# First norm copied once out of PSUM by ACT and DVE in turn, other order of sums and weights, decays one activation at a time

## The chip, the core and the metric

The kernel runs on one core of a Trainium2 chip. Five engines work side by side, each through its own instructions in order: TensorE (PE) multiplies matrices, VectorE (DVE), ScalarE (ACT) and GpSimd (POOL) work on tiles of 128 partitions, and SyncE (SP) issues most of the DMA transfers. They wait for one another by semaphores. The metric is the device time of one execution in microseconds (us), the median of several.

## The reference

One block of a hybrid network on x of 1024 tokens by 1024 features, in fp32. The parts that matter here, cut:

```python
h = rmsnorm(x, norm_mix_pre)                      # x * rsqrt(mean(x*x) + eps) * w
proj = h @ w_in                                   # 1024 x D_IN
(rq, rk, rv, rg, gq, gk, gv, gg, ga, sq, sk, sv, gate_logits) = split(proj)
...                                               # retention of rq, rk, rv
z = ga @ gla_w_alpha2 + gla_b_alpha               # ga: 16 columns, z: 4 heads x 128
log_a = maximum(log_sigmoid(z) / 16, -1)
b = cumsum(log_a)                                 # in each chunk, along the tokens
q_dec, k_inv = q * exp(b), k * exp(-b)            # the decays of the GLA branch
...                                               # GLA, sliding-window attention (sq, sk, sv)
merged = sum(sigmoid(gate_logits) * (branches @ w_branch))
x = x + rmsnorm(merged @ w_out, norm_mix_post)
x = x + rmsnorm(feed_forward(rmsnorm(x, norm_ffn_pre)), norm_ffn_post)
```

## The kernel before

Every fp32 operand is split into two parts, hi (rounded by ACT's copy) and lo (the rest, a subtraction on DVE), and each product is three matmuls: hi hi, hi lo, lo hi. `split(hi, lo, src)` does this for one tile; its two lines are L127 and L128 in the trace.

**The first norm.** x is loaded as eight tiles of 128 tokens, four to a half. `first_norm` squares a tile with a sum (ms), `rstd_of` makes two small POOL instructions of it (add eps, power of -0.5), and DVE scales the tile (xn). TensorE transposes xn in pieces of 128 columns into banks of PSUM (xps), so that bank k holds 128 features of 512 tokens. `first_split` writes the split of such a bank times the norm's weight straight out of PSUM: hi by ACT, lo by DVE (both called hT). `first_whole` writes it once more, whole (hf), on ACT, for the sums of below.

**The products.** All of x's projections come from class `Pairs`, which makes two columns of 128 weights at a time (a key) by seven products instead of eight: p1 to p7, each of four tiles deep, so twelve matmuls of 512 columns. There are 29 keys: one for the keys of sliding-window attention, four for its queries, four for q and k of retention, twenty for gates. The products need sums of the weights (`sums`: s2, s3; DVE subtracts, then a split) and sums of the tiles hf (class `Sums`: t2, t1, t3; `make("t2")` runs them). x, y and z are the banks that products accumulate in. `snap` copies a bank to SBUF (sn) before a later product goes on in it. `out` hands a finished piece to `in_out`, which scales or activates it and stores it. `steps()` is a generator, one `yield` after each product, and the first two keys are taken together.

**The SWA values.** `swa_values(t0)` makes v of the sliding-window attention and ga for two blocks of tokens from the first norm and the weights wsv, which `split_sv` splits in three pieces, the lo part on POOL. `vhl` is the split of its result.

**The decays.** For each of four heads `gla_gate` makes z by one matmul for each half of the tokens (96 deep, the three parts of the split in one), then on ACT exp and ln, on DVE a clamp and a scan along the tokens (cent, with its middle in mid and its end in end), on ACT again exp of end, of mid, and of cent and -cent (ed), which go to DRAM by POOL's queue. exp and ln lie in different tables of ACT, with an ACT_TABLE_LOAD between.

**What sets the order.** Of the first part (from the first norm to `swa_values(6)`) the engines PE, DVE, ACT and POOL keep the order in which the code is written: class `Ordered` marks every instruction issued while `e.on` is true, and all of them have line L76 in the trace. After that, Tile's scheduler orders the instructions, within the waits. The decays are hung into the loop over `steps`: all of a head's work is issued between two products, at steps 10, 17, 24 and 31; `tc.issue_after` keeps the ln after both exp. Tiles named with dt_ come from a pool of 45 buffers of 128 x 1024 fp32, which the weights (raw, wh, wl), x and xn, the sums and the decays (e, cent) share; tiles named with bt come from another of 18 buffers of half that width.

Of the kernel before, what the change touches and what calls it, by code (L numbers as in the profile page):

```python
# [11 lines left out]
AF = mybir.ActivationFunctionType  # L12
ALU = mybir.AluOpType
# [5 lines left out]
D = 1024  # L19
NT = S // P  # L20
NK = D // P
H = 4
# [10 lines left out]
EPS = 1e-6  # L33
# [13 lines left out]
V_PRE, V_RW, V_RB, V_GW, V_FFN, V_BA, V_SNK, V_R, V_CAUSAL = 0, 8, 16, 24, 32, 40, 44, 60, 68  # L47
# [32 lines left out]
def block_kernel(ctx: ExitStack, tc: tile.TileContext, x, vecs, rows, alpha2, w_in, w_branch,  # L80
                 w_out, w_gate, w_up, w_down, cst_in, out):
    nc = tc.nc
    pe, ve, se, po = (Ordered(tc, e) for e in (nc.tensor, nc.vector, nc.scalar, nc.gpsimd))
# [15 lines left out]
    def bt(n, dt=F32):  # L99
        return bp.tile([P, TH], dt, name=f"{n}_{nid()}", tag="b")  # L100
# [7 lines left out]
    def bpair(n):  # L108
        t = dt_(n, F32R)
        return t[:, :TH], t[:, TH:]  # L110
# [21 lines left out]
    vec = const.tile([P, NVEC], F32, name="vec")  # L132
# [45 lines left out]
    def split_sv(raws):  # L178
        res = []
        for raw, kn in raws:  # L180
            wh, wl = wt_pair()
            split(wh[:, :kn * NSV], wl[:, :kn * NSV], raw[:, :kn * NSV], po)
            res += [(wh[:, k * NSV:(k + 1) * NSV], wl[:, k * NSV:(k + 1) * NSV]) for k in range(kn)]
        return res
# [111 lines left out]
            xs.append(xt)  # L296
        return xs

    def first_norm(xt, on_ve):
        xn = dt_("xn")  # L300
        ms = sm("ms", 1)
        if on_ve:
            ve.tensor_tensor_reduce(out=xn, in0=xt, in1=xt, scale=1.0 / D, scalar=0.0,
                                    op0=ALU.mult, op1=ALU.add, accum_out=ms)
        else:
            se.activation(out=xn, in_=xt, func=AF.Square, scale=1.0 / 32.0, accum_out=ms)
        r = rstd_of(ms, 1, EPS)
        ve.tensor_scalar(out=xn, in0=xt, scalar1=r, scalar2=None, op0=ALU.mult)
        return xn

    def first_whole(k, th, ps):
        hf[k][th] = bt("hf")
        se.activation(out=hf[k][th], in_=ps, func=AF.Copy, scale=vec[:, V_PRE + k:V_PRE + k + 1])

    def first_split(k, th, ps):
        xT[k][th] = bpair("hT")
        g = vec[:, V_PRE + k:V_PRE + k + 1]
        se.activation(out=xT[k][th][0], in_=ps, func=AF.Copy, scale=g)
        ve.scalar_tensor_tensor(out=xT[k][th][1], in0=ps, scalar=g, in1=xT[k][th][0],
                                op0=ALU.mult, op1=ALU.subtract)  # L320


    ga = const.tile([P, NT, RANK], F32, name="ga")
# [289 lines left out]
    def gla_gate(h):  # L613
        es, cents = halves(dt_("e")), halves(dt_("cent"))
        mid = const.tile([P, NT], F32, name=f"mid{h}")
        end = const.tile([P, NT], F32, name=f"end{h}")
        for th in range(2):
            ps = bank("z")
            pe.matmul(ps, lhsT=gate_in["a"][:96, h * DK:(h + 1) * DK], rhs=gate_in[th][:96, :],
                      start=True, stop=True)  # L620
            e = es[th]
            ve.tensor_scalar(out=e, in0=ps, scalar1=vec[:, V_BA + h:V_BA + h + 1], scalar2=-25.0,
                             op0=ALU.add, op1=ALU.max)
            last = se.activation(out=e, in_=e, func=AF.Exp, scale=-1.0)
        with tc.issue_after(last.ins):
            for e in es:
                se.activation(out=e, in_=e, func=AF.Ln, bias=1.0)
        for th in range(2):
            e = es[th]
            ve.tensor_scalar(out=e, in0=e, scalar1=-1.0 / 16.0, scalar2=-1.0, op0=ALU.mult, op1=ALU.max)  # L630
            b = cents[th]
            ve.tensor_tensor_scan(out=b, data0=gate_in["scan"], data1=e, initial=0.0, op0=ALU.mult, op1=ALU.add)
            b3 = b.rearrange("p (c t) -> p c t", c=4)
            m_ = mid[:, th * 4:(th + 1) * 4]
            ve.tensor_copy(out=m_, in_=b3[:, :, MID])
            ve.tensor_tensor(out=b3, in0=b3, in1=m_.unsqueeze(2).broadcast_to([P, 4, P]), op=ALU.subtract)
# [61 lines left out]
    xs = load_x(0)  # L698
# [5 lines left out]
    engines = (pe, ve, se, po)  # L704
    for e in engines:
        e.on = True
    xns = [first_norm(xt, False) for xt in xs]
    inp.blocks(ikeys[0])
    pss = [bank("xps") for _ in range(NK)]
    for j in range(4):  # L710
        for k in range(NK):
            pe.transpose(out=pss[k][:, j * P:(j + 1) * P], in_=xns[j][:, k * P:(k + 1) * P], identity=ident)
    for k in range(NK):
        first_split(k, 0, pss[k])
        if k < 2:
            first_whole(k, 0, pss[k])
    wsv = split_sv(wsv)
    next(steps)
    next(steps)
    xns = [first_norm(xt, j > 1) for j, xt in enumerate(xs2)]  # L720
    for k in range(2, NK):
        first_whole(k, 0, pss[k])
    swa_values(0)
    for k in range(NK):
        ps = bank("xps")
        for j in range(4):
            pe.transpose(out=ps[:, j * P:(j + 1) * P], in_=xns[j][:, k * P:(k + 1) * P], identity=ident)
        first_split(k, 1, ps)
        first_whole(k, 1, ps)
    inp.sums(ikeys[0])  # L730
    swa_values(2)
    inp.blocks(ikeys[1])
    next(steps)
    next(steps)
    swa_values(4)
    swa_values(6)
    for e in engines:
        e.on = False
    del xs, xs2, xns, pss
    wsv = None  # L740
    for k in range(KH):
        for z in range(2):
            po.dma_start(out=hTd[k][:, z * TH:(z + 1) * TH], in_=xT[k][1][z].bitcast(F32))
        xT[k][1] = None
    for i, _ in enumerate(steps):
# [18 lines left out]

    dist = bt("dist")[:, :2 * W]
    sp.dma_start(out=dist, in_=cst_in[:, C_DIST:C_DIST + 2 * W])
    po.tensor_scalar(out=nsnk, in0=snk, scalar1=-1.0, scalar2=None, op0=ALU.mult)


    keys, queries, biases = {}, {}, {}  # L770
# [620 lines left out]
```

## Time and profile before

| | |
|---|---|
| median of 3 runs | 2230.72 us (2230.05 to 2232.22) |
| the profiled execution | 2227.39 us, its span 2225.6 us |
| TensorE's granted clock, mean over the span | 0.98 |
| PE busy | 2118.2 us, 95% of the span, 10660 matmuls |
| DVE busy | 1202.5 us, 54% |
| ACT busy | 917.1 us, 41% |
| POOL busy | 241.0 us, 11% |
| DMA | 364.06 MB, mean 164 GB/s |

The profile is of one execution. Its own time stands beside the span since the time holds a little work around the span. Busy shares are averages over stages: in the first tenth of the span PE is busy for half to nine tenths of each slice, later for nearly all. Times within the trace count from the start of the span. "Idle before <- releaser" says how long the engine waited ahead of an instruction, and for whose instruction.

### The profile page before, as it was taken

The numbers are of one execution on the slowest core, as the hardware profiler recorded it, in microseconds if no ns is written. First come the engines' busy times: TensorE is split into PE (matmuls) and PEld (weight loads), VectorE is DVE, ScalarE is ACT, GpSimd is POOL, SyncE is SP. The second block draws the span as 40 slices with busy tenths as digits, with TensorE's granted clock in tenths as the row PEclk, the third lists the DMA queues.
The fourth block names the chain that finished last, engine by engine and source line by source line (L and its number), as shares of the span: only waits on it lengthen the run. The fifth ranks groups of instructions, "written<-read, shape, count | busy, mean of one in ns | idle before, by whom it ended". The sixth has DMA issues, their size and how long they took to land. (4 is left out here: it accounts for less than half of the span.)

```text
span 2225.6 us, 28749 instructions
## 1 busy us (share of the span) xinstructions
PE 2118.2 (95%) x10660; PEld 1792.9 (81%) x10660; DVE 1202.5 (54%) x2215; ACT 917.1 (41%) x1776; POOL 241.0 (11%) x413
## 2 busy tenths in 40 slices
PE   5688999999999999999989999998899999999998
PEld 5567788888889999999967888877688888878786
DVE  3666754444427986655554344426565555544351
ACT  5345444444437775444333212145433333333140
POOL 3011000000012222333321000031000000000000
PEclk9898999999999999999999999999999999999999
DMA  5277655555575446766564535332365555464451
GB/s 184 68 218 224 204 172 161 163 163 166 169 221 173 145 148 210 259 218 204 190 255 156 160 110 156 104 122 87 89 171 142 139 140 142 127 239 164 152 189 38
DMA packets 343277, 364.06 MB, mean 164 GB/s; under 512 B 16464, under 2 KB 267728, under 8 KB 343136
## 3 DMA queue, kind: packets, MB, share of 16 engines
q1 hardware_dynamic: 299776, 265.20, 39.6%
q10 hardware_dynamic: 30816, 54.02, 6.6%
q0 software_dynamic: 12544, 43.00, 5.0%
q8 instruction: 84, 1.38, 0.3%
q14 instruction: 57, 0.47, 0.1%
HBM read 264.64 MB, written 97.52 MB: 163 GB/s over the span
## 5 line engine op out<-in xcount | busy, mean ns | idle before, releaser
L128 DVE TENSOR_TENSOR wl<-raw,wh 128x1024 fp32r<-128x1024 f32 x131 | 160.1, 1223 | 158.2 <-ACT wh L127 80.8
L127 ACT CAST s<-raw 128x512 fp32r<-128x512 f32 x202 | 122.5, 620 | 243.1 <-DVE raw L384 79.8
L127 ACT CAST wh<-raw 128x1024 fp32r<-128x1024 f32 x141 | 147.3, 1047 | 155.0 <-DMA raw<-in_w_down 55.2
L409 PE MATMUL x<-t,s 128*128 128x512 f32 x408 | 161.7, 401 | 21.4 <-ACT sn L359 12.6
L410 PE MATMUL x<-t,s 128*128 128x512 f32 x408 | 163.1, 400 | 0.9 <-DVE t L128 0.7
L411 PE MATMUL x<-t,s 128*128 128x512 f32 x408 | 162.3, 398 | 0.0
L242 PE MATMUL pf<-o,wh 128*128 128x512 f32 x384 | 148.1, 393 | 8.4 <-ACT o L127 8.4
L243 PE MATMUL pf<-o,wh 128*128 128x512 f32 x384 | 149.7, 392 | 0.2 <-DVE o L128 0.2
L359 ACT COPY sn<-x 128x512 f32<-128x512 f32 x151 | 88.4, 586 | 144.5 <-PE x L411 134.9
L257 PE MATMUL v<-wh,hT 128*128 128x256 f32 x512 | 146.4, 286 | 0.0
L259 PE MATMUL v<-wh,hT 128*128 128x256 f32 x512 | 145.4, 284 | 0.0
L258 PE MATMUL v<-wl,hT 128*128 128x256 f32 x512 | 145.4, 284 | 0.0
L1322 PE MATMUL dn<-wh,f 128*128 128x512 f32 x352 | 137.0, 392 | 3.7 <-ACT f L127 3.7
L128 DVE TENSOR_TENSOR s<-raw,s 128x512 fp32r<-128x512 f32 x202 | 136.2, 688 | 2.1 <-ACT s L127 1.5
L1323 PE MATMUL dn<-wl,f 128*128 128x512 f32 x352 | 137.1, 391 | 0.0
L245 PE MATMUL pf<-o,wl 128*128 128x512 f32 x384 | 121.1, 390 | 0.0
L1191 POOL TENSOR_TENSOR rr<-rr,mhalf 128x1 f32<-128x1 f32 x16 | 8.7, 541 | 959.4 <-DVE rr L1190 959.4
L409 PEld LDWEIGHTS x<-t,s 128*128 128x128 f32 x408 | 78.7, 194 | 40.7 <-ACT sn L359 14.3
L1325 PE MATMUL dn<-wh,f 128*128 128x512 f32 x352 | 109.1, 390 | 0.0
L257 PEld LDWEIGHTS v<-wh,hT 128*128 128x128 f32 x512 | 98.7, 193 | 1.2
L258 PEld LDWEIGHTS v<-wl,hT 128*128 128x128 f32 x512 | 98.8, 193 | 1.1
L259 PEld LDWEIGHTS v<-wh,hT 128*128 128x128 f32 x512 | 98.7, 193 | 0.1
(303 smaller groups left out, 5365.8 us busy)
## 6 DMA issues: line engine op xcount, KB each, us to landing
raw<-in_w_in SPq DMA_DIRECT2D x138, 512.0 KB, 6.1
raw<-in_w_down SPq DMA_DIRECT2D x44, 512.0 KB, 6.8
raw<-in_w_gate SPq DMA_DIRECT2D x43, 512.0 KB, 4.8
raw<-in_w_up SPq DMA_DIRECT2D x43, 512.0 KB, 4.7
v<-v POOLq DMA_DIRECT2D x32, 512.0 KB, 4.0
v<-v SPq DMA_DIRECT2D x32, 512.0 KB, 6.5
gT<-go ACTq DMA_DIRECT2D x48, 256.0 KB, 3.9
raw<-in_w_branch SPq DMA_DIRECT2D x24, 512.0 KB, 6.0
```

The lines of the kernel that those rows point to most:

```text
L127: se.copy(out=hi, in_=src)
L128: return (eng or ve).tensor_tensor(out=lo, in0=src, in1=hi, op=ALU.subtract)
L242: pe.matmul(p_, lhsT=wh, rhs=hi, start=(k == 0), stop=False)
L243: pe.matmul(p_, lhsT=wh, rhs=lo, start=False, stop=False)
L257: pe.matmul(ps, lhsT=lh, rhs=rh, start=start, stop=False)
L258: pe.matmul(ps, lhsT=lh, rhs=rl, start=False, stop=False)
L259: pe.matmul(ps, lhsT=ll, rhs=rh, start=False, stop=stop)
L409: pe.matmul(ps, lhsT=h, rhs=hi, start=(start and k == 0), stop=False, skip_group_check=True)
L410: pe.matmul(ps, lhsT=h, rhs=lo, start=False, stop=False, skip_group_check=True)
L411: pe.matmul(ps, lhsT=l, rhs=hi, start=False, stop=(k == KH - 1), skip_group_check=True)
L1322: pe.matmul(ps[ch], lhsT=fh[:, ts_], rhs=ws[ch][0], start=(first and i == 0), stop=False)
L1323: pe.matmul(ps[ch], lhsT=fh[:, ts_], rhs=ws[ch][1], start=False, stop=False)
```

## The change

In the first norm:

- `first_norm` is taken apart into `first_square` and `first_scale`. All eight squares are on ACT now (before, two of them were on DVE), four of them between the tiles of the first half.
- `first_whole` is gone. `first_split` copies a bank out of PSUM once, whole, to hf: even k on ACT, odd k on DVE. The split is made from hf in SBUF, hi on ACT and lo on DVE.
- `split_sv` (the SWA weights) is written after the first two products instead of before them.
- `blocks` of the second key (the cast of its weights) is written between the tiles of the second half. The second key's sums and t2 are put in front of `swa_values(4)` and (6).
- nsnk, a small POOL instruction that needs vec and that only the attention reads later, is put at the end of the ordered part.

In the decays, `gla_gate` becomes a generator with a `yield` behind each activation or pair of them, and `all_decays` runs the four heads one behind the other. The loop over `steps` takes one piece after each product from step 9 on; `issue_after` chains each activation to the end of the one kept in `last`.

```diff
-    def first_norm(xt, on_ve):
+    def first_square(xt):
...
-        if on_ve:
-            ve.tensor_tensor_reduce(out=xn, in0=xt, in1=xt, scale=1.0 / D, scalar=0.0,
-                                    op0=ALU.mult, op1=ALU.add, accum_out=ms)
-        else:
-            se.activation(out=xn, in_=xt, func=AF.Square, scale=1.0 / 32.0, accum_out=ms)
-        r = rstd_of(ms, 1, EPS)
+        se.activation(out=xn, in_=xt, func=AF.Square, scale=1.0 / 32.0, accum_out=ms)
+        return xn, rstd_of(ms, 1, EPS)
+
+    def first_scale(xt, xn, r):
         ve.tensor_scalar(out=xn, in0=xt, scalar1=r, scalar2=None, op0=ALU.mult)
         return xn
...
     def first_split(k, th, ps):
+        h = hf[k][th] = bt("hf")
+        g = vec[:, V_PRE + k:V_PRE + k + 1]
+        if k % 2:
+            ve.tensor_scalar(out=h, in0=ps, scalar1=g, scalar2=None, op0=ALU.mult)
+        else:
+            se.activation(out=h, in_=ps, func=AF.Copy, scale=g)
         xT[k][th] = bpair("hT")
-        g = vec[:, V_PRE + k:V_PRE + k + 1]
-        se.activation(out=xT[k][th][0], in_=ps, func=AF.Copy, scale=g)
-        ve.scalar_tensor_tensor(out=xT[k][th][1], in0=ps, scalar=g, in1=xT[k][th][0],
-                                op0=ALU.mult, op1=ALU.subtract)
+        split(*xT[k][th], h)
...
             last = se.activation(out=e, in_=e, func=AF.Exp, scale=-1.0)
-        with tc.issue_after(last.ins):
-            for e in es:
-                se.activation(out=e, in_=e, func=AF.Ln, bias=1.0)
+            yield
+        for e in es:
+            with tc.issue_after(last.ins):
+                last = se.activation(out=e, in_=e, func=AF.Ln, bias=1.0)
+            yield
...
             ve.tensor_copy(out=end[:, th * 4:(th + 1) * 4], in_=b3[:, :, P - 1])
-        se.activation(out=end, in_=end, func=AF.Exp)
-        se.activation(out=mid, in_=mid, func=AF.Exp)
+            yield
+        with tc.issue_after(last.ins):
+            se.activation(out=end, in_=end, func=AF.Exp)
+            se.activation(out=mid, in_=mid, func=AF.Exp)
+        yield
...
-                se.activation(out=o, in_=cents[th], func=AF.Exp, scale=sgn)
+                with tc.issue_after(last.ins):
+                    se.activation(out=o, in_=cents[th], func=AF.Exp, scale=sgn)
                 po.dma_start(out=ed[h][z][:, th * TH:(th + 1) * TH], in_=o)
+                yield
...
     for k in range(NK):
         first_split(k, 0, pss[k])
-        if k < 2:
-            first_whole(k, 0, pss[k])
-    wsv = split_sv(wsv)
+        if k % 4 == 3:
+            sq += [first_square(xt) for xt in xs2[k // 2 - 1:k // 2 + 1]]
+    xns = [first_scale(xt, *q) for xt, q in zip(xs2, sq)]
     next(steps)
     next(steps)
-    xns = [first_norm(xt, j > 1) for j, xt in enumerate(xs2)]
-    for k in range(2, NK):
-        first_whole(k, 0, pss[k])
+    wsv = split_sv(wsv)
     swa_values(0)
...
         first_split(k, 1, ps)
-        first_whole(k, 1, ps)
+        if k == 3:
+            inp.blocks(ikeys[1])
     inp.sums(ikeys[0])
     swa_values(2)
-    inp.blocks(ikeys[1])
     next(steps)
     next(steps)
+    inp.sums(ikeys[1])
+    inp.make("t2")
     swa_values(4)
     swa_values(6)
+    po.tensor_scalar(out=nsnk, in0=snk, scalar1=-1.0, scalar2=None, op0=ALU.mult)
...
-        if i in (10, 17, 24, 31):
-            gla_gate(len(gates_gla))
+        if i > 8:
+            next(decays, None)
```

DVE, where key 1's sums and t2 stand against the SWA values of the last four blocks. raw_215 and raw_216 are key 1's weights, s its sums, t those of the tiles hf; vhl_687 and vhl_745 (before) are the last two results of `swa_values`, vhl_601 (after) is that of `swa_values(2)`. Before:

```order
L76 TENSOR_TENSOR wl_606<-raw_215,wh_605 128x1024
L384 TENSOR_TENSOR raw_215<-raw_215,raw_216 128x512
L388 TENSOR_TENSOR raw_216<-raw_216 128x512
L76 TENSOR_TENSOR vhl_687<-sv_637,vhl_687 128x4x64
L76 COPY ga<-sv_637 128x16
L76 TENSOR_TENSOR vhl_687<-sv_638,vhl_687 128x4x64
L76 COPY ga<-sv_638 128x16
L76 TENSOR_TENSOR vhl_745<-sv_695,vhl_745 128x4x64
L76 COPY ga<-sv_695 128x16
L128 TENSOR_TENSOR s_118_762<-raw_215,s_118_762 128x512
L76 TENSOR_TENSOR vhl_745<-sv_696,vhl_745 128x4x64
L76 COPY ga<-sv_696 128x16
```

After:

```order
L76 TENSOR_TENSOR vhl_601<-sv_551,vhl_601 128x4x64
L76 COPY ga<-sv_551 128x16
L76 TENSOR_TENSOR vhl_601<-sv_552,vhl_601 128x4x64
L76 COPY ga<-sv_552 128x16
L76 TENSOR_TENSOR raw_215<-raw_215,raw_216 128x512
L76 TENSOR_TENSOR s_112_638<-raw_215,s_112_638 128x512
L76 TENSOR_TENSOR raw_215<-raw_216,raw_215 128x512
L76 TENSOR_TENSOR s_113_642<-raw_215,s_113_642 128x512
L76 TENSOR_TENSOR raw_216<-raw_216 128x512
L76 TENSOR_TENSOR raw_215<-raw_215 128x512
L76 TENSOR_TENSOR t_114_647<-hf_506,hf_462 128x512
L76 TENSOR_TENSOR t_114_647<-t_114_647,hf_291 128x512
```

The sums of key 1 and the first of t2 have moved in front of the last two SWA results, and the key's wl has moved up among the tiles, out of these rows.

ACT, at the end of the first head's decays: sn_1346 (before) and sn_1328 (after) are the same copy of bank x after p6 of the fourth key, wh_1348 and wh_1335 the next key's weights, ed the decays. Before:

```order
L643 ACT_TABLE_LOAD
L643 ACTIVATE ed_1250<-cent_1225 128x512
L675 ACTIVATE qs_1315<-sn_1125 128x512
L127 CAST s_217_1320<-raw_1022 128x512
L679 DMA sq_151<-qs_1315 128x512
L639 ACTIVATE mid_1226<-mid_1226 128x8
L638 ACTIVATE end_1227<-end_1227 128x8
L643 ACTIVATE ed_1253<-cent_1225 128x512
L643 ACTIVATE ed_1256<-cent_1225 128x512
L643 ACTIVATE ed_1259<-cent_1225 128x512
L127 CAST a22h_1298<-raw_1023 128x512
L359 COPY sn_1346<-x_1206 128x512
```

After:

```order
L127 CAST s_213_1297<-raw_1023 128x512
L683 DMA sq_151<-qs_1292 128x512
L356 COPY sn_1328<-x_1215 128x512
L640 ACT_TABLE_LOAD
L640 ACTIVATE mid_1209<-mid_1209 128x8
L639 ACTIVATE end_1210<-end_1210 128x8
L127 CAST wh_1335<-raw_1110 128x1024
L356 COPY sn_1376<-x_1215 128x512
L646 ACTIVATE ed_1384<-cent_1208 128x512
L127 CAST s_223_1355<-raw_1110 128x512
L356 COPY sn_1400<-x_1387 128x512
L646 ACTIVATE ed_1405<-cent_1208 128x512
```

The copy sn has moved in front of the table load and of all ed, and the four ed lie apart, with casts and copies between them.

PE, at the first gate product: z<-g,a is the first half of the first head; x_967 (before) and x_968 (after) are the bank of the third key in its product p4 with a22, and x_1215 is the next key's bank, whose product stands in front of p4 before. Before:

```order
L411 MATMUL x_967<-b_930,a22l_1095 128x512
L409 MATMUL x_967<-b_933,a22h_1094 128x512
L410 MATMUL x_967<-b_933,a22h_1094 128x512
L411 MATMUL x_967<-b_933,a22l_1095 128x512
L619 MATMUL z_1228<-g_192_1158,a_190_1148 128x512
L409 MATMUL x_967<-b_936,a22h_1094 128x512
L410 MATMUL x_967<-b_936,a22h_1094 128x512
```

After:

```order
L408 MATMUL x_968<-b_931,a22l_1096 128x512
L406 MATMUL x_968<-b_934,a22h_1095 128x512
L616 MATMUL z_1211<-g_192_1159,a_190_1149 128x512
L406 MATMUL x_1215<-hT_293,wh_1128 128x512
L407 MATMUL x_1215<-hT_293,wh_1128 128x512
L408 MATMUL x_1215<-hT_293,wl_1129 128x512
L406 MATMUL x_1215<-hT_298,wh_1128 128x512
```

Seven matmuls of the product with a22 now stand in front of the gate product, where nine of it and the next key's twelve stood.

## Rows read from the trace of the kernel before

**Rows 1.** Busy time of each engine by stretches, columns as in the first row

```profile
core 0: us, PE busy (x) PEld busy (x) DVE busy (x) ACT busy (x) POOL busy (x), PEclk, DMA share, GB/s
160.00:170.00 10.00, 3.21 (x9) 2.38 (x8) 7.42 (x14) 6.03 (x12) 3.78 (x7) 0.78 1.02 330
400.00:650.00 250.00, 250.00 (x1105) 207.01 (x1104) 112.67 (x161) 107.60 (x172) 4.78 (x2) 1.00 0.57 172
```

**Rows 2.** Waits of PE, first 110 us: line, releaser, us in total, times, longest

```profile
PE x L409 <- ACT t L127: 5.6, 1, 5.6
PE z L409 <- ACT s L127: 4.9, 1, 4.9
PE x L76 <- ACT wh L76: 4.5, 1, 4.5
...
PE x L76 <- DVE wl L76: 1.2, 1, 1.2
```

**Rows 3.** Timeline, 0 to 20 us: start, us, engine, line, operation, idle before

```profile
9.15 1.06 ACT L76 ACTIVATE xn<-x 128x1024 f32<-128x1024 f32 x1
9.53 0.29 POOL L767 TENSOR_SCALAR nsnk<-vec 128x16 f32<-128x16 f32 x1 [8.71 <-DMA vec<-in_vecs]
...
14.77 0.57 POOL L76 TENSOR_TENSOR rstd<-rstd,mhalf 128x1 f32<-128x1 f32 x1
...
16.55 0.69 ACT L76 ACTIVATE hT<-xps,vec 128x512 fp32r<-128x512 f32 x1 [4.22 <-PE xps L76]
```

**Rows 4.** Timeline of ACT and DVE, first tile of the second half

```profile
39.71 0.69 ACT L76 ACTIVATE hT<-xps,vec 128x512 fp32r<-128x512 f32 x1 [2.17 <-PE xps L76]
...
40.43 0.75 DVE L76 SCALAR_TENSOR_TENSOR hT<-xps,vec,hT 128x512 fp32r<-128x512 f32 x1 [0.31 <-ACT hT L76]
...
41.21 0.69 ACT L76 ACTIVATE hf<-xps,vec 128x512 f32<-128x512 f32 x1 [0.82 <-DVE hT L76]
41.80 0.68 ACT L76 ACTIVATE hT<-xps,vec 128x512 fp32r<-128x512 f32 x1
```

**Rows 5.** Timeline, 25 to 57 us: single instructions of POOL, DVE and ACT

```profile
25.14 5.10 POOL L76 TENSOR_TENSOR wl<-raw,wh 128x816 fp32r<-128x816 f32 x3 [9.80 <-ACT wh L76]
...
55.70 0.68 DVE L76 TENSOR_TENSOR raw<-raw,raw 128x512 f32<-128x512 f32 x1
...
56.42 0.62 ACT L76 CAST s<-raw 128x512 fp32r<-128x512 f32 x1
```

**Rows 6.** Timeline of PE, 102 to 217 us: where it waits

```profile
102.13 0.80 PE L409 MATMUL z<-t,s 128*128 128x512 f32 x1 [4.88 <-ACT s L127]
...
147.78 0.47 PE L619 MATMUL z<-g,a 96*128 96x512 f32 x1 [1.09 <-DVE g L606]
...
167.04 0.80 PE L409 MATMUL x<-t,s 128*128 128x512 f32 x1 [6.79 <-ACT sn L359]
...
168.06 0.63 PE L411 MATMUL x<-t,s 128*128 128x512 f32 x1
168.49 0.63 PE L409 MATMUL x<-t,s 128*128 128x512 f32 x1
...
192.48 0.50 PE L409 MATMUL x<-t,s 128*128 128x512 f32 x1 [3.12 <-ACT sn L359]
...
216.48 0.60 PE L409 MATMUL x<-t,s 128*128 128x512 f32 x1 [2.52 <-ACT sn L359]
```

**Rows 7.** Timeline of ACT, 155 to 167 us, in the first head's decays

```profile
155.34 1.28 ACT L627 ACT_TABLE_LOAD   x1
156.63 1.16 ACT L627 ACTIVATE e<-e 128x512 f32<-128x512 f32 x2
...
164.35 1.65 ACT L643 ACTIVATE ed<-cent 128x512 f32<-128x512 f32 x3
...
166.41 0.57 ACT L359 COPY sn<-x 128x512 f32<-128x512 f32 x1
```

**Rows 8.** DMA issues: line, queue, count, KB each, median us to landing

```profile
raw<-in_w_in SPq DMA_DIRECT2D x138, 512.0 KB, 6.1
```

More of the change, by code (lines that the diff above doesn't have):

```diff
@@ L297, in load_x @@
         return xs
-    def first_norm(xt, on_ve):
+    def first_square(xt):
         xn = dt_("xn")
         ms = sm("ms", 1)
-        if on_ve:
-            ve.tensor_tensor_reduce(out=xn, in0=xt, in1=xt, scale=1.0 / D, scalar=0.0,
-                                    op0=ALU.mult, op1=ALU.add, accum_out=ms)
-        else:
-            se.activation(out=xn, in_=xt, func=AF.Square, scale=1.0 / 32.0, accum_out=ms)
-        r = rstd_of(ms, 1, EPS)
+        se.activation(out=xn, in_=xt, func=AF.Square, scale=1.0 / 32.0, accum_out=ms)
+        return xn, rstd_of(ms, 1, EPS)
+    def first_scale(xt, xn, r):
         ve.tensor_scalar(out=xn, in0=xt, scalar1=r, scalar2=None, op0=ALU.mult)
         return xn
-    def first_whole(k, th, ps):
-        hf[k][th] = bt("hf")
-        se.activation(out=hf[k][th], in_=ps, func=AF.Copy, scale=vec[:, V_PRE + k:V_PRE + k + 1])
     def first_split(k, th, ps):
+        h = hf[k][th] = bt("hf")
[4 more added lines that the diff above has]
+            se.activation(out=h, in_=ps, func=AF.Copy, scale=g)
         xT[k][th] = bpair("hT")
-        g = vec[:, V_PRE + k:V_PRE + k + 1]
-        se.activation(out=xT[k][th][0], in_=ps, func=AF.Copy, scale=g)
-        ve.scalar_tensor_tensor(out=xT[k][th][1], in0=ps, scalar=g, in1=xT[k][th][0],
-                                op0=ALU.mult, op1=ALU.subtract)
+        split(*xT[k][th], h)
     ga = const.tile([P, NT, RANK], F32, name="ga")
@@ L706, in block_kernel @@
         e.on = True
-    xns = [first_norm(xt, False) for xt in xs]
+    xns = []
+    for xt in xs:
+        xns.append(first_scale(xt, *first_square(xt)))
     inp.blocks(ikeys[0])
@@ L712, in block_kernel @@
             pe.transpose(out=pss[k][:, j * P:(j + 1) * P], in_=xns[j][:, k * P:(k + 1) * P], identity=ident)
+    sq = []
     for k in range(NK):
         first_split(k, 0, pss[k])
-        if k < 2:
-            first_whole(k, 0, pss[k])
-    wsv = split_sv(wsv)
+        if k % 4 == 3:
+            sq += [first_square(xt) for xt in xs2[k // 2 - 1:k // 2 + 1]]
+    xns = [first_scale(xt, *q) for xt, q in zip(xs2, sq)]
     next(steps)
     next(steps)
-    xns = [first_norm(xt, j > 1) for j, xt in enumerate(xs2)]
-    for k in range(2, NK):
-        first_whole(k, 0, pss[k])
+    wsv = split_sv(wsv)
     swa_values(0)
@@ L728, in block_kernel @@
         first_split(k, 1, ps)
-        first_whole(k, 1, ps)
+        if k == 3:
+            inp.blocks(ikeys[1])
     inp.sums(ikeys[0])
     swa_values(2)
-    inp.blocks(ikeys[1])
     next(steps)
     next(steps)
+    inp.sums(ikeys[1])
+    inp.make("t2")
     swa_values(4)
     swa_values(6)
+    po.tensor_scalar(out=nsnk, in0=snk, scalar1=-1.0, scalar2=None, op0=ALU.mult)
     for e in engines:
         e.on = False
-    del xs, xs2, xns, pss
+    del xs, xs2, xns, pss, sq
     wsv = None
@@ L744, in block_kernel, with all_decays @@
         xT[k][1] = None
+    def all_decays():
+        for h in range(H):
+            yield from gla_gate(h)
+    decays = all_decays()
     for i, _ in enumerate(steps):
@@ L766, in block_kernel @@
     sp.dma_start(out=dist, in_=cst_in[:, C_DIST:C_DIST + 2 * W])
-    po.tensor_scalar(out=nsnk, in0=snk, scalar1=-1.0, scalar2=None, op0=ALU.mult)
     keys, queries, biases = {}, {}, {}
```

## The prediction

> **What bounds the kernel now.** I read the table by stretches first. Its column for PE says where the end of the run is decided: from 400 to 650 us, and at both sides of that stretch, TensorE is busy for all of the time, one matmul in 250/1105 = 0.226 us, while between 160 and 170 us it is busy for 3.21 us of 10, at 0.78 of its clock [rows 1]. The matmuls are the same in both programs, and from some 260 us on the two programs stand in the same order on every engine. So what TensorE idles less in the first 260 us, the whole run is shorter by, and the change can gain nothing anywhere else. Next the waits of TensorE in the first 110 us say which engine it idles for: the casts of ACT that end the chain of sums (t, s) and the weights of the second key (wh, wl) [rows 2]. Then I went through the timelines, engine by engine, for what stands ahead of these on ACT, DVE and POOL [rows 3 to 5], and for the stalls of TensorE from 100 to 220 us [rows 6] with the rows of ACT before them [rows 7]. Everything below is made against the profiled run, 2227.4 us; the median of the runs shown is 3.3 us above it, which I add at the end.
>
> **The start.** The last of the four sums of squares is there when ACT's square of 9.15 us has been read out, near 10.3 us, but POOL ends the last rstd at 14.77 + 0.57 = 15.3 us, because its first instruction, nsnk, waits 8.71 us for vec and all four rstd stand behind it [rows 3]. With nsnk at the end of the section POOL keeps pace with ACT, and the last rstd comes 1.4 us after the last sum, at 11.7 us: 3.6 us earlier. The row does not show what else POOL would do in these 8.71 us (in both programs one more instruction stands ahead of its first arithmetic, and the trace has no duration for it), so the other bound is a gain of nothing. I take 3.6, since ACT and PE show no other wait at that place. The first copy of a tile then starts at 16.55 - 3.6 = 12.9 us.
>
> **The tiles of the first norm.** Before, a tile of the second half takes 41.80 - 39.71 = 2.09 us: ACT writes hi out of PSUM, DVE the rest, and the whole copy on ACT waits 0.82 us for DVE [rows 4]. Eight tiles are 16.7 us, up to 56.4 us [rows 5]. After, a pair of tiles goes ACT copy 0.69, ACT cast 0.62 [rows 4, 5], DVE subtract 0.68 [rows 5], DVE copy of the odd tile (nearest row: its pass over PSUM, 0.75 [rows 4]), ACT cast 0.62, since DVE's copy of the odd tile stands behind its subtract for the even one. That is 3.36 us less the small overlaps at each start, about 3.3 us a pair instead of 4.2. In the first half two pairs, two squares on ACT and two pairs more end near 30 us, and the split of the SWA weights, which now stands behind the two products, lets POOL write the first wl (5.10 us for three [rows 5], 1.9 for the first) only by 34.5 us. The values of SWA are 48 matmuls of 272 columns, in proportion 0.12 us each and twice that after a stall, so some 8 us, and, with the transposes behind them, the first tile of the second half starts at 43.5 us instead of 39.71 [rows 4]: this part alone **loses 3.8 us**. The second half (13.2 us, and 0.95 us for the cast of key 1's weights in its middle) ends at 58 us.
>
> **Key 1, its sums and t2.** Before, x of key 1 waits 4.5 us for wh and 1.2 us for wl [rows 2]; after, both are done in the middle of the tiles. The products start as TensorE comes to them, about 57 us, last 24 x 0.226 = 5.4, and the last 96 matmuls of the SWA values (12.1 us) end at 75 us. Before, DVE then makes the rest of key 1's sums and t2, because they stand behind the SWA values; PE waits 5.6 us for t [rows 2]. After, DVE starts on them at 58: six sums of key 0 and six of key 1, each waiting twice for ACT's cast (5.3 us a key), 0.8 us of SWA values between, and t2 with its share of t1, twenty instructions of 0.6 us (0.68 less the overlap [rows 5]): 12.1 us and 1.2 at its start. 58.3 + 5.3 + 0.8 + 5.3 + 13.3 = 83 us, and t2's product ends at 84.5 us. The next product, z, started at 102.13 us after 4.88 us of waiting for ACT's s [rows 6]. After, ten instructions of ACT stand between t2's product and that cast (two sn, two qs, a22, four t1, s1), 0.54 us each (0.62 less the overlap [rows 5]), 5.4 us: z starts near 90 us. **The first part is worth 102.1 - 90 = 12 us**, less 0.5 for a lo that comes late: 11.6. Its bounds are 8 (no gain at the start) and 15 (ACT and DVE overlap two pairs).
>
> **The decays.** Each head's work was issued in one piece. Its three ed and a pair of small exponentials (164.35, 1.65 us for three) stand on ACT before the copy sn at 166.41 us, for which x of the next key waits 6.79 us [rows 6, 7]. With the next two heads the wait is 3.12 and 2.52 us [rows 6]. After each stall TensorE runs at the lower of its two levels, 1.2 GHz, 168.49 - 168.06 = 0.43 us a matmul instead of 0.23 [rows 1, 6], for twelve, nine and eight matmuls: 29 x 0.20 = 5.8 us. After, sn stands ahead of the table load and of the exponentials, and one ed lies in each step of TensorE of 12 x 0.226 = 2.7 us; ACT is free for half of it. All of it goes: 12.4 + 5.8 = **18.2 us gained**. What is late next: the first gate product waits for g and a, 1.09 us at 147.78 [rows 6]. It now stands fourteen matmuls earlier, 14 x 0.226 = 3.2 us, and its inputs (a DMA, two casts, four instructions of DVE) come no sooner. So it waits 4.3 us, and ten matmuls behind it run at 0.43: **5.2 us lost** with 1.1 given back from before in it. Bounds: nothing lost if the scheduler's earlier loads bring a in time, 8 if the second gate product waits too. The table loads are moved ahead of the next key's wh, 1.28 us each [rows 7]; the step has 2.7 us for it, and I allow 0.3 us each at three keys. Sum: 18.2 - 5.2 - 0.9 = 12. Bounds 6 to 17.
>
> **A rule against it.** The load at 155.34 us takes 1.28 us, and the next activation starts at 156.63, 0.01 us later [rows 7]. The Trainium skill, ScalarE: Activation LUTs, section "What ACT_TABLE_LOAD costs", gives a switch 1.28 us and 1.38 us of drain on top. The trace shows the first and not the second. By the page the two loads of each of four heads, now ahead of casts that TensorE needs, would take up to 11 us back, which makes the last of the rivals.
>
> **The rivals.** *Only the first norm pays* (2219 us): the decays' gain is eaten by the gate inputs and by wh of the next key behind table load, mid and end, which wait for DVE's scan. A wait of 4 us at each of three keys would do it. For it: sn was late for just this kind of reason. Against: a step has 2.7 us, and a load is 1.28 [rows 7]. *Only the decays pay* (2214): the start gains nothing (3.6) and TensorE waits for all three wl of POOL (3.2 more than for the first), so the first norm gives 4 or 5. *More* (2197): the gate inputs come in time and pairs of tiles overlap. *Slower* (2236): e and cent of a head are held through eleven steps, 11 x 2.7 = 30 us, instead of three or four, and the next head's follow at once, in the pool that the weights come from; every load of the next keys would then be issued a buffer late. A load takes 6.1 us to land [rows 8], and late by that at six keys it costs 37 us against the 24 gained. It decides from 4 us a key on. Against it: the pool has 45 buffers, and TensorE does not wait for a load in [rows 2] or [rows 6]. That *the change doesn't do what it says* is excluded by the order of the instructions, where sn stands before the load. *The loads cost more than they show* (2218): ACT has 1.38 us less after each of eight loads, and TensorE waits for each; the row of 0.01 us speaks against it.
>
> **How the numbers follow.** 2227.4 - 11.6 - 12 = 2203.8; on the median's scale, 3.3 above, 2207, and the parts' rounding leaves it between 2200 and 2212. Chances: this forecast 0.55, only the first norm 0.13, only the decays 0.13, more 0.09, costlier loads 0.02, slower 0.05, and 0.03 that both parts fail and nothing is left. The range, 2194 to 2222, takes in the first five down to the bounds of each part's costs, some 0.85 in all with the ends of *more* left out. A measurement of this kernel can tell 0.2%, 4.5 us, from no change: faster 0.92, the sum of the first five, same 0.03, slower 0.05.
>
> **What would show it.** Right: the last rstd ends before 12.5 us; a pair of tiles takes 3.3 us; the first tile of the second half starts at 43 to 44 us; x of key 1 does not wait for wh; z of the first keys starts near 90 us; the first gate product waits about 4 us; no wait of x for sn above 1 us from 150 to 260 us; two equal programs from there, shifted by about 24 us. Wrong: rstd still late, POOL's wl late for SWA, waits of x for wh in the place of those for sn, or a load that TensorE waits for.

## The result and the profile after

| | before | after |
|---|---|---|
| median | 2230.39 us (2229.32 to 2232.22, 4 runs) | 2201.36 us (2197.20 to 2205.30, 4 runs) |
| ratio | | 0.9869, 95% interval 0.9849 to 0.9889 |
| the profiled execution | 2227.39 us, span 2225.6 | 2200.43 us, span 2198.7 |
| PE busy | 2118.2 us | 2114.9 us |

The change makes the kernel 29 us faster, 1.3%. The forecast was 2207 us with a range of 2194 to 2222. The time lies in the range, 5.6 us below the forecast: 29 us gained where 24 were worked out.

Both programs issue the same products, so the first instruction of a product tells how far the changed kernel is ahead at that place:

| first instruction of | before, us | after, us | ahead by |
|---|---|---|---|
| x of the first key | 18.80 | 14.13 | 4.7 |
| the SWA values | 29.58 | 31.40 | -1.8 |
| z of the first two keys | 102.13 | 88.82 | 13.3 |
| the transposes for the gates | 138.14 | 124.44 | 13.7 |
| the scores of the attention | 667.94 | 639.27 | 28.7 |
| the values of retention and GLA (kv) | 866.34 | 836.22 | 30.1 |
| the last stage (dn) | 1969.78 | 1942.48 | 27.3 |

13.7 us come from the first norm, 15.0 from the decays, and behind them the distance stays. It moves by one to three us in the later stages, where the programs are the same; it does so in other runs too, up and down, and I have not followed it. Each place is read from one execution: z of the first two keys starts at 88.82, 88.45, 89.26, 88.53 and 90.26 us in five kernels with this first norm (this one and four of the experiments), so a difference of less than some 2 us at a place is not clear of that.

The table by stretches of the changed kernel, columns as in [rows 1]:

```profile
160.00:170.00 10.00, 10.00 (x45) 8.24 (x45) 7.52 (x12) 6.41 (x13) 3.23 (x6) 1.00 0.89 296
300.00:400.00 100.00, 100.00 (x443) 82.81 (x442) 46.77 (x67) 41.71 (x68) 0.00 (x0) 1.00 0.57 173
```

The stretch in which TensorE was busy for 3.21 us of 10 is full, at full clock.

The waits of TensorE in the first 110 us (line, releaser, us in total, times, longest), to set beside [rows 2]. The longest of the kernel before, which those rows leave out:

```profile
PE xps L76 <- DVE xn L76: 13.5, 2, 11.6
```

The changed kernel:

```profile
PE xps L76 <- DVE xn L76: 7.6, 1, 7.6
PE z L406 <- ACT s L127: 6.0, 1, 6.0
PE x L406 <- ACT t L76: 2.2, 2, 1.2
PE sv L76 <- POOL wl L76: 2.1, 1, 2.1
...
PE sv L76 <- ACT wh L76: 1.7, 1, 1.7
```

The wait for the first xn is 4.0 us shorter. wh and wl of key 1 are gone from the list. wh and wl of the SWA weights are new in it, z waits a little longer than before, and t 2.2 us instead of 5.6. All waits of TensorE in the first 260 us add up to 54.8 us before and to 31 us after: some 24 of the 28.7 us by which the scores of the attention start earlier. The rest is for the most part slow matmuls behind those waits, counted below where the prediction is weighed.

The timeline of the start and of the first pairs of the second half, to set beside [rows 3, 4] (start, us, engine, line, operation, idle before):

```profile
10.78 0.57 POOL L76 TENSOR_TENSOR rstd<-rstd,mhalf 128x1 f32<-128x1 f32 x1
...
12.74 0.69 ACT L76 ACTIVATE hf<-xps,vec 128x512 f32<-128x512 f32 x1 [0.69 <-PE xps L76]
...
42.98 0.69 ACT L76 ACTIVATE hf<-xps,vec 128x512 f32<-128x512 f32 x1
43.70 0.62 ACT L76 CAST hT<-hf 128x512 fp32r<-128x512 f32 x1
45.74 0.62 ACT L76 CAST hT<-hf 128x512 fp32r<-128x512 f32 x1 [1.42 <-DVE hf L76]
46.27 0.68 ACT L76 ACTIVATE hf<-xps,vec 128x512 f32<-128x512 f32 x1
```

The last rstd ends at 11.35 us (before 15.34), and the first copy starts at 12.74. A pair takes 46.27 - 42.98 = 3.29 us, of which ACT waits 1.42 for hf: DVE's copy of the odd tile stands behind its subtract.

The timeline of TensorE and of ACT in the first head's decays, to set beside [rows 6, 7]:

```profile
88.82 0.80 PE L406 MATMUL z<-t,s 128*128 128x512 f32 x1 [6.00 <-ACT s L127]
...
134.24 0.47 PE L616 MATMUL z<-g,a 96*128 96x512 f32 x1 [3.45 <-DVE g L603]
...
135.51 0.63 PE L406 MATMUL x<-hT,wh 128*128 128x512 f32 x1
135.94 0.63 PE L407 MATMUL x<-hT,wh 128*128 128x512 f32 x1
...
174.58 0.50 PE L408 MATMUL x<-hT,wl 128*128 128x512 f32 x1 [0.26 <-DVE wl L128]
...
148.63 0.59 ACT L356 COPY sn<-x 128x512 f32<-128x512 f32 x1 [0.85 <-PE x L408]
149.24 1.28 ACT L640 ACT_TABLE_LOAD   x1
151.88 0.21 ACT L640 ACTIVATE mid<-mid 128x8 f32<-128x8 f32 x1 [1.36 <-DVE cent L635]
...
152.20 1.04 ACT L127 CAST wh<-raw 128x1024 fp32r<-128x1024 f32 x1
154.07 0.59 ACT L356 COPY sn<-x 128x512 f32<-128x512 f32 x1 [0.83 <-PE x L408]
```

From z to 260 us TensorE waits five times: for s and for g as the first two waits show, for wl as the third does, and twice for sn, 0.68 us at 128.90 and 0.27 us at 249.21. The two rows behind the gate product start 0.43 us apart, as matmuls at 1.2 GHz do here. sn, which x waited for, now waits for x itself (0.83 <- PE), and the table load, mid and the cast wh behind it are done in time.

### The profile page after: what moved, and what is told of

It reads as the page before. It is cut to its first block, busy times and chain, and to the rows that moved or that the text cites. A ratio compares the mean times of both kernels' runs of the same rounds, so it can differ in the third digit from the quotient of the medians.

```text
span 2198.7 us, 28731 instructions
## 1 busy us (share of the span) xinstructions
PE 2114.9 (96%) x10660; PEld 1789.7 (81%) x10660; DVE 1205.9 (55%) x2219; ACT 914.1 (42%) x1772; POOL 240.9 (11%) x413
## 3 DMA queue, kind: packets, MB, share of 16 engines
q8 instruction: 84, 1.38, 0.3%
## 5 line engine op out<-in xcount | busy, mean ns | idle before, releaser
L406 PE MATMUL x<-t,s 128*128 128x512 f32 x408 | 158.2, 392 | 5.7 <-ACT s L127 2.8
L407 PE MATMUL x<-t,s 128*128 128x512 f32 x408 | 159.7, 391 | 0.5 <-DVE t L128 0.3
L408 PE MATMUL x<-t,s 128*128 128x512 f32 x408 | 159.1, 390 | 0.0
```

The source lines that it names most:

```text
L406: pe.matmul(ps, lhsT=h, rhs=hi, start=(start and k == 0), stop=False, skip_group_check=True)
L407: pe.matmul(ps, lhsT=h, rhs=lo, start=False, stop=False, skip_group_check=True)
L408: pe.matmul(ps, lhsT=l, rhs=hi, start=False, stop=(k == KH - 1), skip_group_check=True)
```

## The experiments

All are against the kernel before on the same chip; the edits are to the changed kernel unless another is named. The theory is the prediction's: idle time of TensorE taken away before 260 us carries to the end, at several places that add up.

**The first norm alone, the decays alone.** The first kernel takes `gla_gate` and the loop over `steps` from the kernel before:

```diff
-        if i > 8:
-            next(decays, None)
+        if i in (10, 17, 24, 31):
+            gla_gate(len(gates_gla))
```

> The first norm of the changed kernel with the decays of the kernel before. Theory (idle time of TensorE before 260 us carries to the end, and the two parts add): z of the first two keys starts near 88.8 us as in the changed kernel, the waits of x for sn near 6.8, 3.1 and 2.5 us are back, and the time is 2230.4 - 13.5 = 2217 us. Rival (the parts interact, so that without the spread decays the norm's gain is swallowed by the same ACT queue): 2224 to 2230 us.

Measured: 2216.61 us, ratio 0.9948 (0.9933 to 0.9963). z of the first keys starts at 88.45 us. The waits of TensorE, first 300 us:

```profile
PE x L406 <- ACT sn L356: 12.8, 4, 6.9
...
PE z L616 <- DVE g L603: 0.9, 1, 0.9
```

The second is the kernel before with the new `gla_gate` and the new loop:

> The first norm of the kernel before with the spread decays. Theory (parts add): z of the first keys at 102.1 us as before, no wait of x for sn above 1 us from 150 to 260 us, a wait of 3 to 4 us for g at the first gate product, and 2230.4 - 15 = 2215.5 us. Rival (the parts interact): less than 8 us gained, 2222 us or more.

Measured: 2212.20 us, ratio 0.9929 (0.9914 to 0.9944). z starts at 102.25 us. Its waits:

```profile
PE x L409 <- ACT t L127: 5.6, 1, 5.6
...
PE z L619 <- DVE g L606: 3.4, 1, 3.4
...
PE x L409 <- ACT sn L359: 0.9, 2, 0.7
```

Each part brings back or takes away its own waits and leaves those of the other as they were. 0.9948 x 0.9929 = 0.9877, inside the interval of the change, 0.9849 to 0.9889. The parts add, and the rival in which one eats the other falls.

**nsnk in front again.**

```diff
+    po.tensor_scalar(out=nsnk, in0=snk, scalar1=-1.0, scalar2=None, op0=ALU.mult)
     xns = []
     for xt in xs:
         xns.append(first_scale(xt, *first_square(xt)))
...
     swa_values(6)
-    po.tensor_scalar(out=nsnk, in0=snk, scalar1=-1.0, scalar2=None, op0=ALU.mult)
```

> The changed kernel with nsnk again in front of the first rstd on POOL. Theory (the wait for vec sat on the path): the last rstd ends near 15.3 us, the first copy of a tile starts 3.5 to 4 us later, all of it carries to the end: 2205 us against 2201.4. Rival (the later tiles wait for something else, the split of the SWA weights or POOL, which swallows the late start): 2201 to 2202 us, with the first tile of the second half at 43 us as in the changed kernel.

Measured: 2204.32 us, ratio 0.9895 (0.9878 to 0.9911), 2.6 thousandths more than the change; the two intervals overlap. The trace decides. POOL, and ACT at the first tile of the second half:

```profile
9.27 0.29 POOL L76 TENSOR_SCALAR nsnk<-vec 128x16 f32<-128x16 f32 x1 [8.44 <-DMA vec<-in_vecs]
...
46.70 0.69 ACT L76 ACTIVATE hf<-xps,vec 128x512 f32<-128x512 f32 x1
```

That tile starts 46.70 - 42.98 = 3.7 us later, z at 92.55 us instead of 88.82, the scores of the attention are 4.8 us behind the changed kernel, and the last stage 3.5. The late rstd costs about what was forecast for it, 3.6, and nothing behind it is seen to take it up.

**Copies ahead of the splits.** Both tiles of a pair are copied out of PSUM before either is split; what is left of the old `first_split` above these lines is now `first_copy`, the copy alone:

```diff
-        xT[k][th] = bpair("hT")
-        split(*xT[k][th], h)
+
+    def first_split(k, th, ps):
+        first_copy(k, th, ps)
+        if k % 2:
+            for j in (k - 1, k):
+                xT[j][th] = bpair("hT")
+                split(*xT[j][th], hf[j][th])
```

> The changed kernel with both copies of a pair of tiles out of PSUM written ahead of both splits, so that DVE's copy of the odd tile no longer stands behind its subtract for the even one. Theory (the order on DVE makes the pair 3.3 us): a pair takes DVE's three passes, about 2.0 us, in both halves; 4 x 1.2 us in the second half carry to the end, and as much in the first half less the POOL split behind it: 2192 to 2196 us. Rival (ACT and DVE slow each other when both read PSUM, or the pair is bound by the hand-overs): a pair stays at 3 us or more and the time at 2200 to 2202 us.

Measured: 2191.99 us, ratio 0.9835 (0.9820 to 0.9850). ACT and one row of DVE, first pair of the second half:

```profile
38.41 0.69 ACT L76 ACTIVATE hf<-xps,vec 128x512 f32<-128x512 f32 x1
38.85 0.75 DVE L76 TENSOR_SCALAR hf<-xps,vec 128x512 f32<-128x512 f32 x1
39.13 1.14 ACT L76 CAST hT<-hf 128x512 fp32r<-128x512 f32 x2
40.18 0.68 ACT L76 ACTIVATE hf<-xps,vec 128x512 f32<-128x512 f32 x1
```

The pair takes 40.18 - 38.41 = 1.8 us, the later ones of the second half 2.0 to 2.6. Here both casts run without a wait between them; in the later pairs the second waits 0.2 to 0.7 us for DVE. z starts at 79.60 us, 9.2 earlier than in the changed kernel. So the 3.3 us of a pair are the order on DVE. The two engines' copies overlap for 0.25 us in this pair and in no other of the second half, so what reading PSUM at the same time costs is not shown.

**The weights of the gates earlier.** al and a in a function of their own, at step 5:

```diff
-    def gla_gate_inputs():
+    def gla_gate_weights():
...
+        if i == 5:
+            gla_gate_weights()
         if i == 8:
             gla_gate_inputs()
```

> The changed kernel with the small weights of the gates (al, a) loaded and split at step 5 instead of 8, g as before. Theory (what the spread decays cost is the wait of the first gate product for a's DMA and its chain, and the matmuls at 1.2 GHz behind it): the wait of 3.45 us for g goes and with it the slow matmuls, 2.0 us; 5 us in all, 2196 us. Rival (the wait is the g chain, which lies behind other work of ACT and DVE): the wait stays above 2 us and the time at 2200 to 2201.

Measured: 2197.61 us, ratio 0.9855 (0.9841 to 0.9870). TensorE at the first gate product:

```profile
128.51 0.39 PE L619 MATMUL z<-g,a 96*128 96x512 f32 x1
129.34 0.50 PE L406 MATMUL x<-b,a22h 128*128 128x512 f32 x1 [0.45 <-ACT sn L356]
```

The gate product waits for nothing (it also stands seven matmuls earlier), and TensorE stays at full clock behind it. At the scores of the attention this kernel is 3.5 us ahead of the changed one; 5 were expected. The medians differ by 3.7 us, but the intervals overlap. Together with the copies first the gain is clearer; that run follows below.

**No second table.** exp in place of ln in the decays (which then are no longer the reference's):

```diff
-                last = se.activation(out=e, in_=e, func=AF.Ln, bias=1.0)
+                last = se.activation(out=e, in_=e, func=AF.Exp, scale=-0.01)
```

> The changed kernel with exp in place of ln in the decays, so that ACT needs no second table there: eight table loads fewer, and the decays are not the reference's. Theory (a load is 1.28 us of ACT, which is free for it, and nothing more): TensorE's waits before 260 us stay as they are within 0.5 us, 2200 to 2202 us. Rival (a load costs a drain too and holds up casts that TensorE needs): 5 to 11 us less, 2190 to 2196.

Measured: 2199.90 us, ratio 0.9868 (0.9854 to 0.9883). The waits of TensorE from 100 to 300 us:

```profile
PE z L616 <- DVE g L603: 3.1, 1, 3.1
PE x L406 <- ACT sn L356: 0.7, 1, 0.7
```

They are the same as in the changed kernel within 0.4 us, though ACT_TABLE_LOAD now stands in the trace once instead of nine times. Between the first gate product and the scores of the attention this kernel gains 0.7 us on it. Eight loads cost TensorE less than a us in all. Of the drain that the Trainium skill adds to a load (ScalarE: Activation LUTs, "What ACT_TABLE_LOAD costs") nothing is seen here either.

**The split of the SWA weights earlier.**

```diff
         first_split(k, 0, pss[k])
+        if k == 5:
+            wsv = split_sv(wsv)
...
     next(steps)
-    wsv = split_sv(wsv)
```

> The changed kernel with the split of the SWA weights written between the sixth and seventh tile of the first half instead of behind the two products. Theory (the first half loses since POOL's wl comes late): the two waits of sv for wh (1.7) and wl (2.1) go, the last tiles come about 1 to 2 us later, the first tile of the second half starts 2 to 3 us earlier than 43.0 us, and 2198 to 2199.5 us. Rival (ACT is the bound of the first half, so that each of the casts only moves the tiles behind it): no gain, 2201 to 2203.

Measured: 2200.80 us, ratio 0.9868 (0.9853 to 0.9883): no difference to the change. DVE and ACT at the last pair of the first half, and the stretch around the gate product, of this kernel and (last row) of the changed one, columns as in [rows 1]:

```profile
28.59 1.83 DVE L76 TENSOR_TENSOR hT<-hf,hT 128x512 fp32r<-128x512 f32 x1 [2.63 <-ACT hT L76]
...
31.12 0.62 ACT L76 CAST hT<-hf 128x512 fp32r<-128x512 f32 x1 [2.56 <-DVE hf L76]
```

```profile
125.00:145.00 20.00, 15.69 (x55) 12.13 (x55) 13.20 (x22) 9.99 (x17) 1.62 (x3) 0.83 0.36 103
```

```profile
125.00:145.00 20.00, 15.87 (x64) 12.38 (x62) 13.62 (x25) 9.70 (x17) 1.08 (x2) 0.91 0.42 136
```

The waits for wh and wl of the SWA weights, 3.8 us, go. But their casts now stand on ACT between the tiles, 2.19 us, as the theory allowed for, and POOL's wl runs beside the last pair: DVE's subtract for the even tile takes 1.83 us instead of 0.69, and ACT waits 2.56 us instead of 1.42 for the odd tile behind it. So 1.9 us of the 3.8 are left at the second half (41.08 against 42.98; the theory had 2 to 3) and 2.6 at the first gate product. There nearly the same wait, 3.63 us, is followed by thirteen matmuls at 0.43 us instead of nine: 0.83 of the clock in the stretch instead of 0.91. At the scores of the attention 0.8 us is left. The theory had the place right and not the price.

**One piece, new chain.** The new `gla_gate` run to its end at steps 10, 17, 24 and 31:

```diff
-        if i > 8:
-            next(decays, None)
+        if i in (10, 17, 24, 31):
+            run(gla_gate(len(gates_gla)))
```

> The changed kernel with all of a head's decays issued in one step again (steps 10, 17, 24, 31), the chain of the activations kept as the change has it. Theory (it is the spread over the steps that lets sn go ahead): the waits of x for sn near 6.8, 3.1 and 2.5 us are back, the wait for g is about 1 us, 2215 to 2217 us. Rival (the chain by which each activation follows the last one does it): 2200 to 2204 us.

Measured: 2215.57 us, ratio 0.9942 (0.9926 to 0.9959).

```profile
PE x L406 <- ACT sn L356: 12.8, 4, 6.9
...
PE z L616 <- DVE g L603: 1.1, 1, 1.1
```

The waits are those of the decays before, one by one (6.88, 3.12, 2.56 and 0.20 us for 6.79, 3.12, 2.52 and 0.21). It is the spread over the steps, not the chain of the activations.

**What is left: four more.** The two edits that gained, together:

> Both earlier edits together: the copies of a pair of tiles ahead of their splits, and the small weights of the gates at step 5. Theory (idle time of TensorE taken away at two places before 260 us adds): the ratios of the two, 0.9835 and 0.9855 against 0.9869 of the change, multiply to 0.9821, that is 2189 us. Rival (with the norm 9 us earlier the gate inputs wait for something else): the wait of the first gate product is back at 2 us or more, 2192 us.

Measured: 2186.20 us, ratio 0.9803 (0.9786 to 0.9821). They add, and gain some 3 us more than their ratios give (2189 was expected); each of the four times lies below every time of the copies first alone. TensorE waits no more at the gate product. Then the casts that z of the first keys waits for, 5 to 6 us in the kernels so far, were moved ahead:

```diff
     inp.make("t2")
+    for n in ikeys[:2]:
+        inp.split(n, "s1")
+    inp.make("t1")
     swa_values(4)
...
```

> As the one before, and s1 of both first keys and t1 written behind t2 in the ordered part, so that ACT has their casts done before the product of t2 ends. Theory (z of the first keys waits 6 us because ten other instructions of ACT stand ahead of its cast): that wait goes, z starts 6 to 8 us earlier, of which 2 to 3 us come back as a wait for t3 on DVE: 2183 to 2185 us. Rival (DVE's chain of subtracts is the bound there, whatever ACT does): z starts at most 2 us earlier, 2188 to 2190 us.

Measured: 2185.49 us, ratio 0.9798 (0.9783 to 0.9813), no gain: 0.7 us less than the run before. The time is near the theory's and its mechanism is wrong. z starts at 74.43 us instead of 78.06, but the first product with a22, further on, at 92.42 instead of 91.97. DVE in between:

```profile
75.44 0.69 DVE L76 TENSOR_TENSOR hf<-hf,t 128x512 f32<-128x512 f32 x1
76.16 0.69 DVE L76 TENSOR_TENSOR t<-hf,t 128x512 f32<-128x512 f32 x1
77.54 0.69 DVE L76 TENSOR_TENSOR t<-t,t 128x512 fp32r<-128x512 f32 x1 [0.68 <-ACT t L76]
78.14 0.68 DVE L76 TENSOR_TENSOR hf<-hf,t 128x512 f32<-128x512 f32 x1
```

Each t1 takes 2.7 us there: two subtracts, 0.68 us of waiting for ACT's cast, and the subtract that needs it. ACT was not the bound behind z's first cast, DVE was. So the next kernel writes another sum between each cast and its subtract (in `sums`, `t2` and `t1`; here t1):

```diff
-                res.append(moving("t1", t2))
+                if not ve.on:
+                    res.append(moving("t1", t2))
+                    continue
+                pr = bpair("t1")
+                se.copy(out=pr[0], in_=t2)
+                if k:
+                    ve.tensor_tensor(out=res[-1][1], in0=self.t[k - 1][1], in1=res[-1][0], op=ALU.subtract)
+                res.append(pr)
...
```

> As the run with t1 ahead, and on DVE a subtract or an add of the next sum written between each cast of ACT and the subtract that needs it (key sums, t2, t1). Theory (DVE's chain bounds this stretch, and 0.7 us of it at each cast is waiting for ACT): some ten gaps of 0.7 us go, four of them hidden behind the SWA values; x of the product with a22 starts near 88 us instead of 92.4, 2180 to 2182 us. Rival (the chain is bound by DVE's busy time or by TensorE itself): less than 1.5 us earlier, 2184 to 2186 us.

Measured: 2179.35 us, ratio 0.9770 (0.9750 to 0.9789). The product with a22 starts at 84.57 us, 7.9 earlier, where 88 was expected: the direction of the theory held, and it had the gain too small. This is the fastest of all by its median, 1% below the changed kernel. Last, two of the sums of each key and one of each t1 on POOL, eight passes in all (here that of t1):

```diff
-                ve.tensor_tensor(out=b21, in0=b21, in1=t2, op=ALU.subtract)
+                (po if po.on else ve).tensor_tensor(out=b21, in0=b21, in1=t2, op=ALU.subtract)
```

> As the one before, and eight of the passes (two sums of each of the two keys, one of each t1) on POOL, which is idle there. Theory (DVE's busy time is what is left): 2 to 4 us less again than the run before, 2177 to 2180 us. Rival (TensorE is the bound by now, or POOL's slower passes are waited for): the same as the run before within 1 us.

Measured: 2182.52 us, ratio 0.9790 (0.9770 to 0.9810). The median is 3.2 us longer than that of the run before, but the intervals overlap, and the two profiled executions are equal, 2180.99 and 2181.06 us. The product with a22 starts at 87.47 us, 2.9 later, and the scores of the attention 2.6 later; in the last stage nothing of it is left. So the 2 to 4 us forecast did not come, and whether the whole run is longer stays open. POOL and DVE of this kernel, then DVE of the run before:

```profile
55.42 1.38 DVE L76 TENSOR_TENSOR s<-raw,s 128x512 fp32r<-128x512 f32 x1 [0.69 <-ACT s L76]
...
60.85 1.68 POOL L76 TENSOR_TENSOR hf<-hf,t 128x512 f32<-128x512 f32 x1 [1.95 <-DVE t L76]
63.16 1.67 POOL L76 TENSOR_TENSOR hf<-hf,t 128x512 f32<-128x512 f32 x1 [0.63 <-DVE t L76]
...
61.41 1.67 DVE L76 TENSOR_TENSOR t<-t,hf 128x512 f32<-128x512 f32 x1
...
63.61 1.78 DVE L76 TENSOR_TENSOR t<-hf,hf 128x512 f32<-128x512 f32 x1
```

```profile
54.56 0.69 DVE L76 TENSOR_TENSOR s<-raw,s 128x512 fp32r<-128x512 f32 x1
...
59.32 0.69 DVE L76 TENSOR_TENSOR t<-t,hf 128x512 f32<-128x512 f32 x1
```

A pass of DVE that starts while POOL works takes 1.67 or 1.78 us instead of 0.69, or 1.23 to 1.38 us beside POOL's shorter passes in the key sums: it ends half a us behind POOL's. There is a second loss. In the key sums the passes that went to POOL were those that filled DVE's wait for ACT's cast, and the wait of 0.69 us is back at four casts. DVE has fewer passes and is no sooner through. Both expectations missed this; the rival named POOL's slow passes, but not that DVE stands still for them.

## Why the prediction was right, and where it was short

- **The bound.** Right. TensorE's waits before 260 us, with the slow matmuls behind them, set the gain: the two programs are 28.7 us apart when the attention begins and 27.3 in the last stage. The prediction's list of waits left out the longest, 13.5 us for xn; its term for the start covers most of what changed there.
- **The start.** Right: the last rstd at 11.35 us for 11.7 (the last sum was there 0.3 us earlier than before), and the run with nsnk in front shows that the 3.6 us count at the tiles and at z. The lower bound, no gain, is excluded.
- **The tiles.** Right: a pair at 3.29 us for 3.3, the first tile of the second half at 42.98 for 43.5. TensorE waits for SWA's wl there, 2.1 us, as forecast, and 1.7 for wh, which I had not named. Where I allowed a gain from overlap of two pairs, there is none in this order; the copies written first show what the order costs, 9 us.
- **Key 1, sums and t2.** Right in place, 1.7 us short in size: z starts at 88.82 us for "near 90", 13.3 gained for 11.6. DVE starts on the sums 0.5 us earlier than forecast; t2 takes 12.3 us for 13.3, since the 1.2 at its start was already in the sums of key 1; the product of t2 ends 0.25 sooner behind it; the ten instructions of ACT before z take 6.0 us for 5.5; and the 0.5 for a lo that comes late was not needed. Which share the single copy out of PSUM has in the 13.3 us, and which the order of key 1's weights, sums and t2, no run separates: it is read from the waits alone.
- **The decays.** Right in mechanism: the waits for sn go, the wait for g grows from 1.09 to 3.45 us (4.3 forecast), and nine matmuls behind it run at 1.2 GHz (ten forecast). The term is short by 3 us, 15.0 for 12. The gate product costs 4.0 us for 5.2, of which 2.4 are longer waiting and 1.6 slow matmuls. Of the 0.9 allowed for wh behind table loads one wait of 0.26 came. The slow matmuls that go cost 6.0 us for 5.8. And I had left out three small waits of the kernel before, which go as well (the two below and one of 0.21 for sn), against the two new ones for sn of 0.68 and 0.27:

```profile
238.48 0.50 PE L409 MATMUL x<-hT,wh 128*128 128x512 f32 x1 [0.53 <-ACT wh L127]
239.74 0.50 PE L411 MATMUL x<-hT,wl 128*128 128x512 f32 x1 [0.53 <-DVE wl L128]
```

  This makes up 2.4 of the 3 us; the rest I have not traced.
- **The rivals.** *Only the first norm* and *only the decays* are excluded by the two single parts. *Costlier loads* falls with the run without the second table. *Slower*, by late weights, does not appear: TensorE waits for no load in this stretch. (Its price did not follow from its own sum: 37 us late on 2207 would be 2244 and not 2236.) *More* named the right places to look, the gate inputs and the overlap of two pairs, but neither came in the changed kernel; both came in the experiments.

What was off is thus the size of two terms, both too small, and no cause was wrong; the time came out at the lower edge of the 2200 to 2212 that the forecast allowed.

## What to carry to other kernels

Where one engine is full for most of the run, add up its idle time in the stretch that the change touches, name the instruction that each wait ends with, and price each by its row: parts that remove different waits then add. When one of two engines that work on a tile in turn has two jobs there, look at which stands first: written as copy, copy, split, split a pair took 1.8 to 2.6 us, as copy, split, copy, split 3.3. Work that is hung between the steps of a full engine should be cut as small as a step leaves room for; in one piece it stands ahead of the one copy that the full engine needs next.

## What the runs showed of the hardware

- A pass of DVE with two inputs in SBUF, started while POOL adds or subtracts two tiles of SBUF, lasts until after the end of POOL's instruction: 1.67 and 1.78 us for 0.69, and 1.83 beside the split of the SWA weights. The Trainium skill, SBUF — State Buffer, section "Who interferes with whom", says that a DVE instruction with two SBUF inputs contends with a GpSimd instruction that reads SBUF; these traces agree. In the changed kernel a pass with one tile as input met the same: xn, started 0.07 us behind POOL's first wl, took 2.39 us where the one before it took 0.75. I moved work to stand beside POOL's in two runs without weighing it, and both missed their gain.

```profile
31.97 5.53 POOL L76 TENSOR_TENSOR wl<-raw,wh 128x816 fp32r<-128x816 f32 x3
32.04 2.39 DVE L76 TENSOR_SCALAR xn<-x,rstd 128x1024 f32<-128x1024 f32 x1 [0.76 <-POOL rstd L76]
```

- Nearly the same wait can cost more in slow matmuls behind it: nine of 0.43 us after 3.45 us of waiting in the changed kernel, thirteen after 3.63 us in the kernel with the early split. What decides between them these runs do not show.
